# Encoder layer on one core: w_down with 20 pairs of K-tiles in seven-product form, and a tail that adds to seeded banks

## The chip, the cores and the metric

The kernel runs on one core of a Trainium2 chip, in one launch. The metric is the device time of one execution in microseconds (us). TensorE (PE) multiplies, VectorE (DVE), ScalarE (ACT) and GpSimd (POOL) work element by element, SyncE (SP) issues DMAs, and DMA queues are issued by SP, ACT and POOL. Each engine works off its own list of instructions, and semaphores hold an instruction until its inputs are there. SBUF is the memory on the chip, with 128 partitions; the matmuls write into eight PSUM banks of 128x512 numbers each; DRAM is outside.

## The reference

One encoder layer in f32 on 512 tokens of width 2048. What matters here is its last part:

```python
h = rmsnorm(x, ffn_norm_w[l])
x = x + (jax.nn.silu(h @ w_gate[l]) * (h @ w_up[l])) @ w_down[l]     # w_gate, w_up 2048x5632, w_down 5632x2048
...
return rmsnorm(x, final_norm_w)
```

Ahead of it stand w_in, windowed attention, gated linear attention and w_out. g below is silu(gate) times up, 512 tokens by 5632. Along w_down's rows (K) it has 44 K-tiles of 128, or 22 pairs of K-tiles.

## The kernel before, in words

Each f32 operand of a matmul is split into a high and a low part (`hi` is a cast on ACT, `lo` a subtraction on DVE), and each product becomes three matmuls: high by high, high by low, low by high. That is the conventional form: one K-tile, 128 tokens and 512 columns take 3 matmuls of 128x512.

The seven-product form (Winograd's variant of Strassen's scheme) multiplies blocks of 2 by 2 with seven products instead of eight. Sums and differences of blocks are made ahead on both sides, and the seven product sums (m) are combined at the end.

- **gate/up** (class `Feed`, built on `Units`): 22 pairs j, a gate unit and an up unit each, with seven steps a unit. The weights are split in steps by `lead` (L1541 sums, L1566 casts, L1572 subtractions). At the end of an up unit, `finish` multiplies gate and up (L1735 and L1742, 128x1024 on DVE) and POOL writes g of the pair to DRAM as `gd[j]` (L1744).
- **w_down, first part**: four jobs, one for each 512 columns c, on K-tiles 0 to 3 in conventional form (L348 to L350). Their results are multiplied by the norm's factor and added to the residual stream in DRAM (`xd`) by POOL DMAs.
- **w_down, seven-product part** (class `Down`): 16 pairs in four chunks, K-tiles 4 to 35. A chunk has 28 steps of 12 matmuls (L2073 to L2075): two column halves C, seven products, two duos of pairs. `make` reads g back from `gd` on SP and makes the operands T13, T24, F2 and B11 with their high and low parts (L1981 to L1997). After a product's last duo, `evac` copies its two banks to SBUF (L2118, L2120), and a POOL DMA adds them to `md` in DRAM. In the last chunk `fetch` reads `md` back, `put_back` copies it into the banks before the product starts (L2109, L2111), and the sums end in SBUF. `combine` (L2142) then makes the outputs y from the seven sums.
- **w_down, later jobs**: four jobs on K-tiles 36 to 39, conventional, on banks that `seed` has filled with y (L2159 on ACT). `residual` (L1897 on DVE) multiplies a bank by the norm's factor and adds it to x1 in SBUF.
- **tail** (`finish`, its function `run`): K-tiles 40 to 43, conventional. For each 128 tokens t and each 512 columns c there is a group of 12 matmuls (L2288 to L2290) on an empty bank, then `residual` (L1897), then `squares` (L523, ACT, with the row sum read out). After the four groups of a t, `later` makes the reciprocal root (L384 on DVE, L387 and L388 on ACT, L390 to L393 on DVE), scales (L2279) and writes out. The last group (t = 3, c = 3) goes in two halves of 256 columns (`last`, L2303 to L2322).

Nothing reorders instructions: each engine's order is the order in which the code issues them. Work slots in SBUF come from two pools, `s2` (128x512, 36 of them, tiles named a) and `s4` (128x1024, 33, named b). PSUM banks (`ps`) are given out in turn. In the trace a tile is named by the letter of its pool.

## Time and profile before

| | |
|---|---|
| median of 3 runs | 2141.14 us (2140.68 to 2141.53) |
| profiled execution, its own time | 2141.47 us |
| its span | 2139.7 us |
| gate/up to its end | 1695.7 us from the span's start |
| w_down, K-tiles 0 to 3 | 1695.7 to 1739.2 |
| w_down, seven-product part | 1739.3 to 2043.9 |
| w_down, K-tiles 36 to 39 | 2043.9 to 2088.0 |
| tail, K-tiles 40 to 43 | 2088.1 to 2131.9 |
| last output written | 2139.7 |

The stages are read off PE's timeline, by the lines of its matmuls. In the rows that follow, "L2290" is a line of the code above, "ps<-b,a" are the tiles written and read, and a row of the timeline begins with the start, counted from the span's start, and the duration. A row of the groups by line has the shapes, the count, and behind the bars the busy time in us and the mean of one in ns, then the idle time of the engine just ahead of them and what ended it.

### The profile page before, as it was taken

What the parts mean: (1) busy time and instruction counts of PE and PEld (TensorE: products, weight loads), DVE (VectorE), ACT (ScalarE), POOL (GpSimd) and SP (SyncE); (2) the same over time, 40 slices, a digit from 0 to 9 for tenths busy, and PEclk for the clock granted to TensorE, in tenths of its full rate; (3) what the DMA queues carried; (4) which work ended last, traced back from release to release, by engine and by line L of the source; (5) the groups of instructions that cost most, each with busy time, mean ns of one, the idle gap of its engine ahead of it and who ended that gap; (6) DMA issues with size and microseconds to landing.
All of it is one profiled execution on the core that took longest, in us unless ns stands there. A gap on an engine that the chain in (4) does not pass through costs nothing.

```text
span 2139.7 us, 30612 instructions
## 1 busy us (share of the span) xinstructions
PE 2128.3 (99%) x11418; PEld 1831.6 (86%) x11418; DVE 1732.0 (81%) x2361; ACT 1224.1 (57%) x2051; POOL 181.4 (8%) x294
## 2 busy tenths in 40 slices
PE   9999999999999999999999999999999999999998
PEld 7888888888888889988888888888888888888887
DVE  6688888778877568888888888888888888887885
ACT  8454445477776546455555555445555566666762
POOL 0000000122222000000000000000000010332000
PEclk9999999999999999999999999999999999999999
DMA  6644554647664233534444343344343596999572
GB/s 205 178 129 129 141 141 131 190 146 214 186 200 123 92 128 100 152 115 123 124 125 122 109 138 116 114 125 128 115 124 107 193 254 236 209 247 248 189 254 79
DMA packets 340849, 330.46 MB, mean 154 GB/s; under 512 B 15389, under 2 KB 260621, under 8 KB 340702
## 3 DMA queue, kind: packets, MB, share of 16 engines
q1 hardware_dynamic: 313598, 258.07, 39.3%
q0 software_dynamic: 26784, 69.91, 12.7%
q8 instruction: 90, 1.47, 0.3%
q10 hardware_dynamic: 320, 0.53, 0.1%
q14 instruction: 57, 0.47, 0.1%
HBM read 267.55 MB, written 60.92 MB: 154 GB/s over the span
## 4 chain that ended last, share of the span: by engine, by line
PE 95%; DMA 1%; issue 1%; ACT 1%; DVE 1%; POOL 0%; SPq 0%; DVEq 0%; POOLq 0%; ACTq 0%
PE ps L1604 35%; PE ps L1607 18%; PE ps L350 6%; PE ps L349 6%; PE ps L348 6%; PE ps L2074 5%; PE ps L2075 5%; PE ps L2073 5%; PE ps L699 1%; PE ps L2290 1%; PE ps L2289 1%; PE ps L2288 1%; PE ps L643 1%; PE ps L1702 1%; PE ps L1701 1%
## 5 line engine op out<-in xcount | busy, mean ns | idle before, releaser
L1572 DVE TENSOR_TENSOR b<-b,b 128x1024 fp32r<-128x1024 f32 x406 | 496.2, 1222 | 99.8 <-ACT b L1566 98.5
L1566 ACT CAST b<-b 128x1024 fp32r<-128x1024 f32 x406 | 421.2, 1052 | 21.1 <-DMA b<-in_w_in_dram 14.9
L1604 PE MATMUL ps<-a,b 128*128 128x512 f32 x1656 | 424.5, 392 | 0.1
L1604 PE MATMUL ps<-b,b 128*128 128x512 f32 x1592 | 421.0, 393 | 0.0
L1604 PEld LDWEIGHTS ps<-a,b 128*128 128x128 f32 x1656 | 304.4, 188 | 62.6 <-ACT ps L1638 0.3
L1604 PEld LDWEIGHTS ps<-b,b 128*128 128x128 f32 x1592 | 280.3, 189 | 42.5
L1541 DVE TENSOR_TENSOR b<-b,b 128x1024 f32<-128x1024 f32 x232 | 282.8, 1219 | 12.6 <-DMA b<-in_w_in_dram 12.5
L1607 PEld LDWEIGHTS ps<-b,b 128*128 128x128 f32 x1592 | 232.6, 190 | 23.4
L1607 PE MATMUL ps<-b,b 128*128 128x256 f32 x1592 | 242.9, 282 | 0.0
L1607 PE MATMUL ps<-a,b 128*128 128x256 f32 x1656 | 242.6, 283 | 0.0
L1607 PEld LDWEIGHTS ps<-a,b 128*128 128x128 f32 x1656 | 224.7, 191 | 8.3
L1632 ACT COPY b<-ps 128x256 f32<-128x256 f32 x126 | 46.9, 373 | 250.8 <-PE ps L1607 228.8
L2049 DVE TENSOR_TENSOR b<-b,b 128x1024 fp32r<-128x1024 f32 x112 | 136.5, 1221 | 36.0 <-ACT b L2041 36.0
L348 PE MATMUL ps<-b,b 128*128 128x512 f32 x344 | 139.1, 404 | 0.2 <-ACT b L462 0.2
L350 PE MATMUL ps<-b,b 128*128 128x512 f32 x344 | 134.6, 391 | 0.2 <-DVE b L466 0.2
L349 PE MATMUL ps<-b,b 128*128 128x512 f32 x344 | 134.4, 391 | 0.0
L2041 ACT CAST b<-b 128x1024 fp32r<-128x1024 f32 x112 | 116.6, 1052 | 25.4 <-DVE b L2029 13.1
L220 DVE TENSOR_TENSOR b<-b,b 128x512 fp32r<-128x512 f32 x120 | 79.4, 684 | 18.1 <-ACT b L239 17.9
L2073 PE MATMUL ps<-b,a 128*128 128x512 f32 x240 | 93.4, 389 | 0.0
L2074 PE MATMUL ps<-b,a 128*128 128x512 f32 x240 | 93.4, 389 | 0.0
L2075 PE MATMUL ps<-b,a 128*128 128x512 f32 x240 | 93.4, 389 | 0.0
L348 PE MATMUL ps<-a,b 128*128 128x512 f32 x216 | 86.7, 401 | 0.0
(311 smaller groups left out, 3596.4 us busy)
## 6 DMA issues: line engine op xcount, KB each, us to landing
b<-in_w_in_dram SPq DMA_DIRECT2D x94, 512.0 KB, 5.3
b<-in_w_gate_dram SPq DMA_DIRECT2D x88, 512.0 KB, 4.3
b<-in_w_up_dram SPq DMA_DIRECT2D x88, 512.0 KB, 3.8
b<-in_w_down_dram SPq DMA_DIRECT2D x88, 512.0 KB, 7.2
b<-in_w_out_dram SPq DMA_DIRECT2D x32, 512.0 KB, 4.7
md<-a POOLq DMA_DIRECT2D x56, 256.0 KB, 6.9
gd<-b POOLq DMA_DIRECT2D x22, 512.0 KB, 5.3
b<-gd SPq DMA_DIRECT2D x22, 512.0 KB, 5.1
```

Source lines behind the costliest of these rows:

```text
L348: mm(o, xh.t[:, c], wh.t[:, w], start=first and not on, stop=False, skip_group_check=on)
L349: mm(o, xh.t[:, c], wl.t[:, w], start=False, stop=False, skip_group_check=on)
L350: mm(o, xl.t[:, c], wh.t[:, w], start=False, stop=last, skip_group_check=on)
L1541: tt = lambda o, x_, y_: dve.tensor_tensor(o.t, x_.t, y_.t, op=OP.add)
L1566: act.copy(hi.t, home[key].t)
L1572: dve.tensor_tensor(lo.t, home[key].t, hi.f, op=OP.subtract)
L1604: mm(o.rearrange("p (s t) -> p s t", s=2), hi.t[:, q], self.xs[q][self.ORDER[n]], start=new and q == 0, stop=False, skip_group_check=True)
L1607: mm(o[:, 0:256], lo.t[:, q], self.xs[q][self.ORDER[n]][:, 0], start=False, stop=q == NP - 1, skip_group_check=True)
L2049: dve.tensor_tensor(lo.t, s.t, hi.f, op=OP.subtract)
L2073: mm(o, xh[:, t], wh, start=new and j == 0, stop=False, skip_group_check=True)
L2074: mm(o, xh[:, t], wl, start=False, stop=False, skip_group_check=True)
L2075: mm(o, xl[:, t], wh, start=False, stop=last and j == 1, skip_group_check=True)
```

## The change

- w_down's seven-product part takes 20 pairs in five chunks (K-tiles 0 to 39), 140 steps of 12 matmuls. The jobs on K-tiles 0 to 3 and 36 to 39 are gone. The tail keeps K-tiles 40 to 43 in conventional form.
- `prepare` makes the operands of a pair (the arithmetic of the old `make`) and writes high and low parts to DRAM, `gx[j]`, by POOL. For pairs 0 to 11 it runs in gate/up, right behind the product of gate and up, and g itself is not written; for pairs 12 to 19 `make` reads `gd` (now by POOL) and runs it in w_down. `fill` reads the operands back by POOL, kind by kind, as slots come free.
- The product sums stay in SBUF: `evac` copies the banks to `m`, and `put_back` copies `m` into the banks at the start of each product from the second chunk on. `md`, its transfers and `fetch` are gone. The order of the products within a chunk differs.
- In the tail `products` first copies y into the bank on ACT (L2232), and all matmuls add to it. The groups come in the order (t 0, 1 by c 0, 1), (t 0, 1 by c 2, 3), then t 2 and 3.
- x1 is loaded, g's last four K-tiles are split, the final norm's weights are loaded and the tail's weights are split within the last 14 steps (`ending`). The activation table of the reciprocal root is loaded between the last step and the tail.
- Gate/up holds at most 7 raw weight quads instead of 8.

```diff
+PAIRS, EARLY, FEED = 20, 12, 7
...
+        gx = dr.tile([PAIRS, P, 3584], F32, name="gx")
+        def prepare(q, f):
+            n1, f2 = f.t[:, 1], f.t[:, 0]
+            T = two(F32)
+            t13, t24 = T[0].t, T[1].t
+            tt(t13[:, a], n1[:, z], n1[:, a], op=OP.subtract)
+            tt(t13[:, z], f2[:, z], n1[:, z], op=OP.add)
+            tt(t24[:, a], f2[:, z], t13[:, a], op=OP.add)
+            tt(t24[:, z], t24[:, a], f2[:, a], op=OP.subtract)
+            yield
+            for src, col, n, done in ((f2, 512, 512, ()), (n1[:, a], 0, 256, (f,)), (t13, 1536, 512, ()),
+                                      (t24, 2560, 512, T), (None, 0, 0, ())):
...
+                        tt(lo, x_, hf, op=OP.subtract)
...
+                        pool.dma_start(out=d, in_=os_[0].flat)
...
+                    put(*os_, *gone)
...
+                    act.activation(hi, src, AF.Copy, scale=sign)
+                    yield
...
-                    pool.dma_start(out=gd[j], in_=c_.t.rearrange("p f t -> p (f t)"))
-                    put(c_)
+                    if j < EARLY:
+                        yield
+                        yield from prepare(j, c_)
+                    else:
+                        pool.dma_start(out=gd[j], in_=c_.t.rearrange("p f t -> p (f t)"))
+                        put(c_)
...
             def evac(self, ch, C, n, banks):
+                if not ch:
+                    self.m.setdefault(C, {})[n] = two(F32, 1)
+                for bank, y in zip(banks, self.m[C][n]):
...
                     put(bank)
-                    if ch == self.end:
-                        continue
-                    if ch:
-                        pool.dma_start(out=md[14 * C + 2 * n + h], in_=y.t, accum_op=OP.add)
...
-        dn = Down([[2, 4], [6, 8], [10, 12], [14, 16]])
+        dn = Down([[4 * n, 4 * n + 2] for n in range(PAIRS // 4)])
...
+            ORDER = [(t, 2 * C + c) for C in range(2) for t in range(2) for c in range(2)] + \
+                [(t, c) for t in (2, 3) for c in range(4)]
...
             def products(b, t, c, cols):
                 tok = slice(t * P, (t + 1) * P)
+                y = dn.y[c // 2][t // 2][c % 2][t % 2]
+                act.copy(b.t[:, cols], y.t[:, cols])
...
-                    mm(b.t[:, cols], xh.t[:, tok], wh.t[:, cols], start=k == 0, stop=False)
+                    mm(b.t[:, cols], xh.t[:, tok], wh.t[:, cols], start=False, stop=False, skip_group_check=True)
...
+                for t, c in ORDER:
...
+                    products(b, t, c, slice(0, 512))
+                    residual(c, t, b)
+                    squares(c, t, x1[c], ss2 if t < 3 else ss1[:, 0:4], 0 if t == 3 else 4 * t)
```

How the instructions stand now, at three places. ScalarE in the tail before, over the first two token tiles (L523 the squares of a group, L387 and L388 the reciprocal root):

```order
L523 ACTIVATE a_826_19763,small<-a_803_19356 128x512
L523 ACTIVATE a_828_19780,small<-a_807_19458 128x512
L523 ACTIVATE a_830_19797,small<-a_811_19574 128x512
L523 ACTIVATE a_832_19814,small<-a_821_19691 128x512
L387 ACTIVATE small<-small 128x1
L388 ACTIVATE small<-small 128x1
L523 ACTIVATE a_834_19847,small<-a_804_19357 128x512
L523 ACTIVATE a_836_19864,small<-a_808_19459 128x512
```

ScalarE in the tail after, from the fifth group on (L531 the squares, L2232 the copy of y into the next group's bank, L395 and L396 the reciprocal root):

```order
L531 ACTIVATE a_850_20027,small<-a_831_19689 128x512
L2232 COPY ps_746_20030<-b_1700_17172 128x512
L531 ACTIVATE a_852_20045,small<-a_833_19739 128x512
L395 ACTIVATE small<-small 128x1
L396 ACTIVATE small<-small 128x1
L2232 COPY ps_747_20064<-a_758_17071 128x512
L531 ACTIVATE a_854_20079,small<-a_832_19690 128x512
L2232 COPY ps_748_20082<-b_1700_17172 128x512
```

A copy into a bank now stands between the squares of one group and those of the next, and behind the root where there is one. TensorE at the border of two tail groups, with what it waits for, before:

```order
L2288 MATMUL ps_745_19749<-b_2017_19569,b_2022_19606 128x512
L2289 MATMUL ps_745_19749<-b_2017_19569,b_2022_19606 128x512
L2290 MATMUL ps_745_19749<-b_2017_19569,b_2022_19606 128x512
L2288 MATMUL ps_746_19766<-b_2019_19594,b_2005_19489 128x512 [waits DVE_49]
L2289 MATMUL ps_746_19766<-b_2019_19594,b_2005_19489 128x512
```

and after, at the group that the second copy above seeds:

```order
L2240 MATMUL ps_745_20006<-b_2068_19972,b_2033_19665 128x512
L2241 MATMUL ps_745_20006<-b_2068_19972,b_2033_19665 128x512 [waits DVE_49]
L2242 MATMUL ps_745_20006<-b_2068_19972,b_2033_19665 128x512
L2240 MATMUL ps_746_20030<-b_2069_19987,b_2024_19605 128x512 [waits Activation_49]
L2241 MATMUL ps_746_20030<-b_2069_19987,b_2024_19605 128x512 [waits DVE_49]
```

The first matmul of a group waited for DVE, which makes the low parts of the weights; it now waits for ACT, which makes the bank's first content. DVE in a pair of gate/up before, around the product of gate and up (L1742):

```order
L1572 TENSOR_TENSOR b_939_10556<-b_936_10532,b_938_10554 128x1024
L1742 TENSOR_TENSOR b_927_10476<-b_927_10476,b_906_10300 128x1024
L1572 TENSOR_TENSOR b_941_10581<-b_910_10325,b_940_10579 128x1024
L1541 TENSOR_TENSOR b_936_10532<-b_936_10532,b_910_10325 128x1024
L1572 TENSOR_TENSOR b_943_10605<-b_902_10272,b_942_10602 128x1024
```

and after (L1786 is the product, L1616 and L1585 the weights' split and sums, L1333 to L1346 the new work):

```order
L1786 TENSOR_TENSOR b_926_10609<-b_926_10609,b_905_10419 128x1024
L1616 TENSOR_TENSOR b_940_10713<-b_912_10480,b_939_10711 128x1024
L1333 TENSOR_TENSOR a_606_10732<-b_926_10609 128x256
L1334 TENSOR_TENSOR a_606_10732<-b_926_10609 128x256
L1335 TENSOR_TENSOR a_607_10733<-b_926_10609,a_606_10732 128x256
L1336 TENSOR_TENSOR a_607_10733<-a_607_10733,b_926_10609 128x256
L1585 TENSOR_TENSOR b_935_10665<-b_935_10665,b_912_10480 128x1024
L1616 TENSOR_TENSOR b_942_10743<-b_902_10388,b_941_10740 128x1024
L1691 TENSOR_TENSOR ps_445_10770<-a_608_10738,ps_442_10709 128x512
L1616 TENSOR_TENSOR b_946_10774<-b_935_10665,b_945_10772 128x1024
L1346 TENSOR_TENSOR a_610_10762<-b_926_10609,a_609_10761 128x512
```

The operands' sums come ahead of weight splits that stood directly behind the product, and the subtractions follow between later splits.

## The prediction

> **What bounds the kernel now.** I read the page first, for the busiest engine and the chain of waits, then the windows of 50 us for what each stage leaves free, then the timeline where the change cuts in. First the page: TensorE's (PE's) busy time, the shares of the chain, and the issue row of g's write.

> ```profile
> PE 2128.3 (99%) x11418; PEld 1831.6 (86%) x11418; DVE 1732.0 (81%) x2361; ACT 1224.1 (57%) x2051; POOL 181.4 (8%) x294
> ...
> PE 95%; DMA 1%; issue 1%; ACT 1%; DVE 1%; POOL 0%; SPq 0%; DVEq 0%; POOLq 0%; ACTq 0%
> ...
> gd<-b POOLq DMA_DIRECT2D x22, 512.0 KB, 5.3
> ```

> PE is busy 99% of the span and carries 95% of the chain. So the time is the number of matmuls times their pitch, plus the moments in which PE has nothing to start. Both are to be counted. The windows give PE, PEld, DVE, ACT and POOL busy time with instruction counts, the granted clock, the DMA share and GB/s: one stretch of gate/up, two of seven-product w_down, then the jobs on K-tiles 36 to 39 with the start of the tail, and the tail with the end.

> ```profile
> 1300.00:1350.00 50.00, 50.00 (x288) 44.04 (x287) 43.42 (x48) 24.76 (x35) 1.06 (x2) 1.00 0.37 108
> ...
> 1950.00:2000.00 50.00, 50.00 (x222) 41.39 (x222) 35.62 (x32) 34.90 (x51) 7.09 (x9) 1.00 0.97 291
> 2000.00:2050.00 50.00, 50.00 (x222) 41.41 (x221) 38.52 (x45) 39.64 (x62) 2.24 (x4) 1.00 0.60 203
> 2050.00:2100.00 50.00, 49.68 (x219) 40.79 (x218) 39.39 (x63) 24.52 (x48) 0.00 (x0) 1.00 0.45 155
> ```

> PE is full in the first three and loses 0.32 us in the fourth. DVE and ACT have room everywhere, in gate/up DVE the least: 6.6 us of 50.

> **Term 1, matmuls removed.** The pitch of a 128x512 matmul, from the timeline of PE, at the first row of the K-tile 36 to 39 jobs and 60 matmuls later:

> ```profile
> 2043.90 0.39 PE L348 MATMUL ps<-b,b 128*128 128x512 f32 x1
> ...
> 2057.50 0.39 PE L348 MATMUL ps<-b,b 128*128 128x512 f32 x1
> ```

> 13.60 us by 60 is 0.2267 us. Before, w_down's body is 192 matmuls on K-tiles 0 to 3, 112 steps of 12 and 192 on K-tiles 36 to 39: 1728. After, it is 140 steps of 12: 1680. The tail has 192 in both. 48 x 0.2267 = **10.9 us** less.

> **Term 2, a stall that goes.** The 0.32 us stand where the first later weights were split late:

> ```profile
> 2060.22 0.39 PE L348 MATMUL ps<-b,a 128*128 128x512 f32 x1
> ...
> 2060.92 0.50 PE L349 MATMUL ps<-b,a 128*128 128x512 f32 x1 [0.32 <-DVE b L220]
> ...
> 2061.26 0.40 PE L350 MATMUL ps<-b,a 128*128 128x512 f32 x1
> ```

> From start to start it is 0.70 and 0.34 instead of 2 x 0.23, so **0.6 us** goes with those jobs. The row also prices a restart: a matmul that had to wait is followed 0.34 later, 0.11 more than the pitch.

> **Term 3, operands made in gate/up.** For each of the first 12 pairs, after the product of gate and up, DVE gets four 256-wide and three 512-wide operations and one 256-wide subtraction, ACT four casts. The rows of these forms in w_down, with the price of one, and the product of gate and up in two consecutive pairs:

> ```profile
> L1996 ACT CAST a<-a 128x512 fp32r<-128x512 f32 x14 | 8.0, 621 | 0.0
> L1993 ACT ACTIVATE a<-b 128x256 fp32r<-128x256 f32 x11 | 4.6, 419 | 0.0
> ...
> L1997 DVE TENSOR_TENSOR a<-a,a 128x512 fp32r<-128x512 f32 x14 | 9.0, 686 | 4.9 <-ACT a L1996 4.9
> L1994 DVE SCALAR_TENSOR_TENSOR a<-b,a 128x256 fp32r<-128x256 f32 x11 | 4.6, 421 | 3.6 <-ACT a L1993 3.6
> ...
> 1307.34 1.22 DVE L1742 TENSOR_TENSOR b<-b,b 128x1024 f32<-128x1024 f32 x1
> ...
> 1346.45 1.22 DVE L1742 TENSOR_TENSOR b<-b,b 128x1024 f32<-128x1024 f32 x1
> ```

> That is 5 x 0.42 + 3 x 0.69 = 4.2 us of DVE and about 2.3 of ACT (three of 0.62, one of 0.42) in a pair of 39.1 us. DVE's present load there is 43.42/50 x 39.1 = 34.0; with it 38.2, still below 39.1. ACT goes from 19.4 to 21.7. The work hides, on condition that within the one unit where it falls (half a pair: 17.0 + 4.2 = 21.2 against 19.6) the split weights stay ahead; the excess of 1.6 us is less than one step's 2.8 (19.6/7), and a step's weights are split at least one step ahead. The g write on POOL (512 KB, landing in 5.3) becomes 1.75 MB in four to seven issues on the same queue, which holds nothing else there; the DMA engines move 108 GB/s there and 291 in w_down, so there is room. I take 0. If the cover goes, each of 12 pairs pays the 1.6: 0 to 19 us, nearer 0 since DVE's sum fits.

> **Term 4, the body of w_down.** Per two steps (24 matmuls, 5.44 us) ACT has two casts, two seed copies and two evacuations. Before's last chunk has this mix already:

> ```profile
> 1999.95 1.27 ACT L2120 COPY b<-ps 128x512 f32<-128x512 f32 x2 [1.23 <-PE ps L2075]
> 2001.11 1.05 ACT L2041 CAST b<-b 128x1024 fp32r<-128x1024 f32 x1
> 2002.06 1.11 ACT L2111 COPY ps<-b 128x512 f32<-128x512 f32 x2
> 2003.10 1.05 ACT L2041 CAST b<-b 128x1024 fp32r<-128x1024 f32 x1
> 2005.39 0.59 ACT L2120 COPY b<-ps 128x512 f32<-128x512 f32 x1 [1.24 <-PE ps L2075]
> ```

> It idles 1.24 of every 5.44 with PE full. In chunks 1 to 4 it now always looks so, and 8 pairs still made there add 32 casts (18 us) to some 60 pairs of steps, 0.3 each: it fits. DVE at 38.5 of 50 gains nothing on average. The 56 accumulating transfers on POOL, their fetches on SP and K-tile loads of two jobs go; POOL gets the reads of the prepared operands (36.7 MB in all), the reads of g, and the writes of pairs 12 to 19. In bytes, a chunk's weights (8.4 MB) and operands (7.3 MB) in 28 steps (76 us) are 206 GB/s, and the writes and reads of those 8 pairs bring it to some 270, about what the 1950 window moved. On POOL a write stands behind its subtraction and a fill behind the write; slots freed at issue make the next cast wait for a landing of about 5.3 us. Such waits I place at the start (the first weights and operands load together), at a few casts of chunks 0 and 1, and at the last 14 steps, where the combining of the product sums and the splitting of g's last four K-tiles nearly fill DVE. No row shows them; the nearest is the 0.6 us of term 2. Its price by two or three places is **1.5 us**; the ends are 0 and, for 8 pairs at 1.2 us each, 10.

> **Term 5, the seeds of the tail.** This decides. Before, a tail group of 12 matmuls starts on an empty bank. Now ScalarE first copies y into it. ACT works in the order given in the listing: squares of group n (L531), then the seed of group n+1 (L2232). The squares wait for DVE's residual, the residual for the end of group n, and the first matmul of n+1 for the seed. So PE stands idle from the end of one group to the seed of the next, whereas before it ran on. The same links, in before's timeline, around the end of a group:

> ```profile
> 2120.48 0.39 PE L2290 MATMUL ps<-b,b 128*128 128x512 f32 x1
> ...
> 2120.71 0.39 PE L2288 MATMUL ps<-b,b 128*128 128x512 f32 x1
> ...
> 2120.91 0.75 DVE L1897 SCALAR_TENSOR_TENSOR a<-ps,small,a 128x512 f32<-128x512 f32 x1 [1.97 <-PE ps L2290]
> ...
> 2121.69 0.63 ACT L523 ACTIVATE a<-a 128x512 f32<-128x512 f32 x1 [2.00 <-DVE a L1897]
> ...
> 2122.23 0.19 ACT L523 ACTIVATION_READ_ACCUMULATOR a<-a 128x1 f32 x1
> ...
> 2123.07 0.20 ACT L388 ACTIVATE small<-small 128x1 f32<-128x1 f32 x1
> ...
> L1632 ACT COPY b<-ps 128x256 f32<-128x256 f32 x126 | 46.9, 373 | 250.8 <-PE ps L1607 228.8
> ...
> L2111 ACT COPY ps<-b 128x512 f32<-128x512 f32 x24 | 13.3, 590 | 2.3 <-DMA b<-md 2.3
> ...
> L176 ACT ACT_TABLE_LOAD x5 | 6.4, 1283 | 1.3 <-PEq L2378 1.2
> ```

> - An ordinary change: the accumulator is read by 2122.42, the copy ends 0.59 later at 2123.01, and PE is released some 0.04 after (as DVE is after PE: 2120.87 to 2120.91), 2123.05. It would have started at 2120.71. With 0.11 for the restart, 2.45 us. There are 12 such, the last into the half group (a 256-wide copy of 0.37, 0.2 less): 29.2.
> - After the fourth group of a token tile ACT also does the two small steps of the reciprocal root (L388's end, 2123.27) ahead of the seed: 0.85 more, 3.30 x 3 = 9.9.
> - The start: last evacuation (0.6), table load 1.28, copy 0.59, with the handovers and restart 2.9.
> - Between the halves of the last group, residual and squares of half width, rows next:

> ```profile
> 2130.89 0.48 DVE L2303 SCALAR_TENSOR_TENSOR a<-ps,small,a 128x256 f32<-128x256 f32 x1
> ...
> 2131.62 0.28 PE L2290 MATMUL ps<-b,b 128*128 128x256 f32 x1
> 2131.73 0.19 ACT L2307 ACTIVATION_READ_ACCUMULATOR a<-a 128x1 f32 x1
> 2132.01 0.21 ACT L2308 ACTIVATE ss<-ss 128x5 f32<-128x5 f32 x1
> ...
> 2135.00:2136.00 1.00, 0.00 (x0) 0.00 (x0) 0.91 (x2) 0.00 (x0) 0.00 (x0) 0.71 0.61 227
> 2136.00:2137.00 1.00, 0.00 (x0) 0.00 (x0) 0.00 (x0) 0.00 (x0) 0.00 (x0) 0.50 1.02 375
> ```

> From the residual to the end of the small squares 0.35 after 2132.01 it is 1.4, plus 0.4 for the copy and 0.4 for handovers: 2.2.

> The sum is 29.2 + 9.9 + 2.9 + 2.2 = **44.2 us**. It scales with each link; with a place at 2.2 or 2.85 it is 40 or 50. Nothing behind it gives this back: the tail ends the program, and the 7.8 us of the span after PE's last matmul (2131.62 + 0.28) stay as they are.

> That ACT takes no later instruction during such a wait is seen in the squares row: 2.00 us idle, though nothing but its own input held it. [...]

> **Sum.** The profiled run took 2141.47 (span 2139.7 and 1.8 around it), 0.3 over the median of 2141.14. On the median: 2141.1 - 10.9 - 0.6 + 1.5 + 44.2 = **2175.3**.

> **The rivals.**
> - *The seeds are hidden, faster.* It needs ScalarE to run a seed before the squares ahead of it. Without term 5 but for its start it is 2134. From the sum, the change pays while the 17 places cost under 0.6 us each (10.0/17), less than the copy alone. For it: a bank is free long before. Against: the listing's order and the 2.00 us for which the squares wait. 3%; another 2% that it just balances.
> - *A cheaper break*, a residual and a seed that overlap their neighbours' ends: 1.0 to 1.8 us a place, 2147 to 2164. 4%.
> - *The body stalls too*: gate/up late by 1 us in each of 12 pairs, or operands landing late in w_down: 12 to 25 us more, 2187 to 2200. It would need one of the two stages to run late in most pairs. For it: gate/up's DVE would have 0.9 us of 39.1 left. 12%.
> - *The clock falls in the breaks.* The last two rows above show it halved about 2135.4, 3.5 us after the last matmul ended (0.71 in that window is 1.00 for 0.42 us and 0.50 after). The longest break here is 3.3. If it fell in each, a group of 2.72 us would run at half speed: 15 x 2.7 = 41 more, 2216; after the long ones only, about 8 more. 5%. [...]

> **How the numbers follow.** 74% for the forecast, 2165 to 2187 with its own bounds (terms 4 and 5). The range adds the lower part of the stalls: 2165 to 2192 leaves out 7% below and some 11% above. No change means within 0.2%, 4.3 us, about what this measurement can tell: 2%. Faster 3%, slower 95%.

> **What would show it.** In after: idle before PE's L2240 put down to ACT L2232, 40 to 50 us summed over 17 places; L2232 itself starting right behind the squares, and the squares L531 waiting for DVE L1930; the tail from first to last matmul near 85 us (43.5 of matmuls and the breaks); the stretch of w_down before it 381 us with PE full; the clock 1.00 through the tail; the first step of w_down at the same time as now. The forecast is wrong if L2232 starts before the residual of the group ahead, if PE shows gaps above 3 us in w_down, or if w_down begins over 2 us later.

## The result, and the profile after

The changed kernel takes 2226.2 us (2225.8 to 2228.1) against 2140.9 in the runs beside it: 1.040 times as long, 95% interval 1.0382 to 1.0418. The forecast was 2175.3, with 2192 as the upper end: the sign was right, the size was not, since 85 us were lost and 34 foretold.

The profiled execution has a span of 2224.5 us, 84.8 more than before. Its page, PE's busy time and the chain of waits:

```profile
PE 2155.8 (97%) x11370; PEld 1843.8 (83%) x11370; DVE 1755.1 (79%) x2381; ACT 1286.5 (58%) x2152; POOL 237.4 (11%) x442
...
PE 90%; DMA 4%; issue 3%; ACT 2%; DVE 2%; POOL 0%; DVEq 0%; ACTq 0%; POOLq 0%
```

PE now stands idle for 3% of the span, and DMA has 4% of the chain, where it had 1%. The windows of 50 us (columns as before) show where:

```profile
1700.00:1750.00 50.00, 45.61 (x195) 37.35 (x194) 38.21 (x43) 27.32 (x38) 5.42 (x10) 0.93 0.75 261
1750.00:1800.00 50.00, 44.27 (x179) 35.08 (x178) 31.07 (x34) 26.37 (x39) 15.13 (x28) 0.93 0.68 246
...
1950.00:2000.00 50.00, 44.60 (x190) 36.45 (x190) 30.89 (x28) 32.61 (x49) 4.46 (x9) 0.93 0.55 192
...
2100.00:2150.00 50.00, 33.85 (x106) 24.20 (x105) 23.73 (x41) 18.77 (x39) 0.00 (x0) 0.81 0.09 29
2150.00:2200.00 50.00, 33.73 (x94) 24.50 (x92) 14.90 (x31) 9.25 (x25) 0.00 (x0) 0.75 0.17 63
```

A full window of w_down has 222 matmuls. Three have 179 to 195, and the tail has 94 to 106. The column behind POOL's counts is the granted clock: it is below 1.00 in each of these windows, down to 0.75 in the tail. What PE waited for, in total, times and the longest:

```profile
PE ps L2240 <- ACT ps L2232: 38.1, 17, 3.0
PE ps L2087 <- DVE b L2055: 5.6, 3, 4.4
PE ps L2086 <- ACT ps L2104: 5.4, 1, 5.4
PE ps L2086 <- ACT b L2047: 4.5, 2, 3.1
PE ps L1648 <- ACT ps L1689: 2.5, 1, 2.5
PE ps L1648 <- DVE a L1698: 1.5, 1, 1.5
```

The first row is the tail's seeds (17 places, 38.1 us), the next three are w_down, the last two gate/up. With PE's first and last rows of the stages

```profile
1701.83 0.40 PE L2086 MATMUL ps<-b,a 128*128 128x512 f32 x1
...
2106.51 0.39 PE L2088 MATMUL ps<-b,b 128*128 128x512 f32 x1
...
2109.53 0.50 PE L2240 MATMUL ps<-b,b 128*128 128x512 f32 x1 [2.63 <-ACT ps L2232]
...
2215.84 0.41 PE L2242 MATMUL ps<-b,b 128*128 128x256 f32 x1
```

the account by stage is as follows (w_down's body ends one pitch behind its last start, at 2106.74).

| stage, us | before | after | difference | forecast |
|---|---|---|---|---|
| to the end of gate/up | 1695.7 | 1701.8 | +6.1 | 0 |
| w_down ahead of the tail | 392.4 | 404.9 | +12.5 (-11.5 and 24.0 of breaks) | -10.0 |
| tail, with its start | 43.8 | 109.5 | +65.7 | +44.2 |
| behind PE's last matmul | 7.8 | 8.25 | +0.4 | 0 |

### The profile page after: what moved, and what is told of

It reads as the page before. It is cut to its first block, busy times and chain, and to the rows that moved or that the text cites. A ratio compares the mean times of both kernels' runs of the same rounds, so it can differ in the third digit from the quotient of the medians.

```text
span 2224.5 us, 30882 instructions
## 1 busy us (share of the span) xinstructions
PE 2155.8 (97%) x11370; PEld 1843.8 (83%) x11370; DVE 1755.1 (79%) x2381; ACT 1286.5 (58%) x2152; POOL 237.4 (11%) x442
## 4 chain that ended last, share of the span: by engine, by line
PE 90%; DMA 4%; issue 3%; ACT 2%; DVE 2%; POOL 0%; DVEq 0%; ACTq 0%; POOLq 0%
PE ps L1648 33%; PE ps L1651 17%; PE ps L356 5%; PE ps L358 5%; PE ps L357 5%; PE ps L2087 5%; PE ps L2086 5%; PE ps L2088 5%; PE ps L2240 1%; DMA gx<-a 1%; PE ps L707 1%; PE ps L2241 1%; PE ps L2242 1%; PE ps L651 1%; PE ps L1746 1%
## 5 line engine op out<-in xcount | busy, mean ns | idle before, releaser
L1616 DVE TENSOR_TENSOR b<-b,b 128x1024 fp32r<-128x1024 f32 x406 | 495.7, 1221 | 84.5 <-ACT b L1610 82.3
L1610 ACT CAST b<-b 128x1024 fp32r<-128x1024 f32 x406 | 422.3, 1049 | 38.8 <-DMA b<-in_w_in_dram 15.1
L1648 PE MATMUL ps<-a,b 128*128 128x512 f32 x1656 | 425.5, 392 | 0.1
L1648 PE MATMUL ps<-b,b 128*128 128x512 f32 x1592 | 421.6, 393 | 4.0 <-ACT ps L1689 2.5
L1648 PEld LDWEIGHTS ps<-b,b 128*128 128x128 f32 x1592 | 280.4, 189 | 46.9 <-ACT ps L1689 2.7
L1585 DVE TENSOR_TENSOR b<-b,b 128x1024 f32<-128x1024 f32 x232 | 282.6, 1218 | 12.8 <-DMA b<-in_w_in_dram 12.8
L2055 DVE TENSOR_TENSOR b<-b,b 128x1024 fp32r<-128x1024 f32 x140 | 170.7, 1222 | 94.2 <-ACT b L2047 89.0
L2047 ACT CAST b<-b 128x1024 fp32r<-128x1024 f32 x140 | 146.1, 1048 | 32.0 <-DVE b L2035 10.9
L2086 PE MATMUL ps<-b,b 128*128 128x512 f32 x416 | 162.3, 390 | 0.0
L2087 PE MATMUL ps<-b,b 128*128 128x512 f32 x416 | 162.0, 389 | 0.0
L2088 PE MATMUL ps<-b,b 128*128 128x512 f32 x416 | 161.8, 389 | 0.0
L1354 POOL DMA_DIRECT2D gx<-a x112 | 60.6, 543 | 504.2 <-ACT a L1365 346.3
L356 PE MATMUL ps<-b,b 128*128 128x512 f32 x260 | 106.7, 410 | 0.0
L358 PE MATMUL ps<-b,b 128*128 128x512 f32 x260 | 102.1, 393 | 0.0
L357 PE MATMUL ps<-b,b 128*128 128x512 f32 x260 | 101.9, 392 | 0.0
L2116 ACT COPY a<-ps 128x512 f32<-128x512 f32 x100 | 57.8, 587 | 59.9 <-PE ps L2088 43.6
## 6 DMA issues: line engine op xcount, KB each, us to landing
b<-in_w_in_dram SPq DMA_DIRECT2D x94, 512.0 KB, 5.3
b<-in_w_gate_dram SPq DMA_DIRECT2D x88, 512.0 KB, 5.3
b<-in_w_up_dram SPq DMA_DIRECT2D x88, 512.0 KB, 4.8
b<-in_w_down_dram SPq DMA_DIRECT2D x88, 512.0 KB, 5.9
b<-gx POOLq DMA_DIRECT2D x52, 512.0 KB, 7.6
b<-in_w_out_dram SPq DMA_DIRECT2D x32, 512.0 KB, 4.6
```

The source lines that it names most:

```text
L356: mm(o, xh.t[:, c], wh.t[:, w], start=first and not on, stop=False, skip_group_check=on)
L357: mm(o, xh.t[:, c], wl.t[:, w], start=False, stop=False, skip_group_check=on)
L358: mm(o, xl.t[:, c], wh.t[:, w], start=False, stop=last, skip_group_check=on)
L1585: tt = lambda o, x_, y_: dve.tensor_tensor(o.t, x_.t, y_.t, op=OP.add)
L1610: act.copy(hi.t, home[key].t)
L1616: dve.tensor_tensor(lo.t, home[key].t, hi.f, op=OP.subtract)
```

## The experiments

The theories: **A**, the tail's breaks are the waits for the seeds, and the breaks bring the clock down; **E**, in w_down ACT waits for slots whose write to `gx` has not landed; **H**, w_down's start lacks DMA bandwidth; its rival there, the loads lack slots. The runs of the kernel before beside these kernels had medians of 2141.2 to 2141.4.

### The seeds one group ahead

```diff
 for g, (t, c) in enumerate(ORDER):
+    seed(g)
+    seed(g + 1)          # act.copy of y into the next group's bank
     products(...)        # no copy in it
     residual(c, t, b)
     squares(c, t, ...)
```

> The changed kernel with one edit: y is copied into the bank of group n+1 before the matmuls of group n are issued, so on ScalarE the seed stands ahead of group n's squares. Theory A (the wait for the seed makes the breaks, and the breaks make the clock fall): both go, the tail shrinks from 109.5 us to about 48 (43.6 of matmuls, 2.6 of start, one slow clock window at the start at most), the clock is 1.00 from then on, and the time falls by about 61 us to 2165. Rival B (the seeded banks or the late weight splits slow the tail in themselves): PE still waits between groups, for DVE's split weights, and the time stays above 2190. Rival C (the clock falls for its own reason in the tail): breaks gone, clock still halved in many windows, about 2188.

2174.4 us (2171.8 to 2174.9), 51.8 less than the changed kernel. Its clock is 1.00 in the tail but for one stretch of 3.4 us behind the start (0.97 on the mean from 2106.9 to 2165 us, against 0.75 over the changed kernel's tail). So theory A holds in kind: the seeds made the breaks, and the clock came back with them; rival C falls. But 61 were expected, and a part of rival B is true. PE's wait in the tail, and a group border:

```profile
PE ps L2251 <- ACT ps L2240: 10.1, 9, 2.6
```

and its timeline:

```profile
2118.21 0.63 ACT L531 ACTIVATE a<-a 128x512 f32<-128x512 f32 x1 [1.50 <-DVE a L1930]
...
2118.84 0.58 ACT L2240 COPY ps<-a 128x512 f32<-128x512 f32 x1
2119.36 1.13 ACT L247 CAST b<-b 128x512 fp32r<-128x512 f32 x2
2119.47 0.50 PE L2251 MATMUL ps<-b,b 128*128 128x512 f32 x1 [0.38 <-ACT ps L2240]
2120.00 1.29 DVE L228 TENSOR_TENSOR b<-b,b 128x512 fp32r<-128x512 f32 x2 [1.82 <-ACT b L247]
...
2121.21 0.74 DVE L1930 SCALAR_TENSOR_TENSOR a<-ps,small,a 128x512 f32<-128x512 f32 x1
```

A second loop stands behind the first: squares, seed, the casts of two weight splits, their subtractions on DVE, and only then the next residual, which the next squares wait for. It takes 3.8 us a group (2117.43 to 2121.21 from residual to residual), longer than 12 matmuls (2.72).

### The breaks filled with matmuls that nobody reads

```diff
     mm(b.t[:, cols], xl.t[:, tok], wh.t[:, cols], start=False, stop=k == per - 1, ...)
+if cols.start == 0:
+    spare = ps.get()
+    for _ in range(8):
+        mm(spare.t, xh.t[:, tok], wh.t, start=True, stop=True)
+    put(spare)
```

> The changed kernel, seeds as they are, but behind each group of the tail PE runs 8 matmuls of 128x512 into a spare bank that nobody reads (added work, 1.8 us of each break of 2.1). The waits for the seeds stay. Theory A (a window of 3.4 us with too little matmul work halves the next one): the clock stays 1.00 through the tail, a group and its break take 5.07 us instead of 6.6, the tail is about 83 us instead of 109.5 and the time falls by some 26 us to 2200, although 128 matmuls were added. Rival D (the lost time beyond the idle is the restart of a waiting PE, not the clock): no gain, 2226 or somewhat more.

2205.1 us (2201.9 to 2207.0): 21.1 less, with 128 matmuls more. Here is the tail's middle, 80 us of it:

```profile
2110.00:2190.00 80.00, 73.41 (x311) 55.99 (x310) 31.05 (x59) 24.01 (x61) 0.00 (x0) 1.00 0.11 40
```

and the wait for the seeds that is left:

```profile
PE ps L2240 <- ACT ps L2232: 9.2, 15, 2.6
```

The clock is 1.00. The seeds come no sooner: 9.2 us of idle and 16 fillings of 1.81 make 38.2, as before. So of the tail's 65.7 some 21 us were the clock and 38 the idle time at the seeds; the 6 or 7 left, restarts behind 17 breaks among them, were not taken apart. Rival D falls. A row of windows, cut along the clock's own steps, shows in the changed kernel how the clock went; the first number behind the length is PE's busy time:

```profile
2113.79:2117.20 3.41, 1.33 (x6) 0.85 (x5) 1.21 (x2) 2.24 (x5) 0.00 (x0) 1.00 0.00 0
2117.20:2120.61 3.41, 3.41 (x9) 2.35 (x8) 0.84 (x2) 0.03 (x1) 0.00 (x0) 0.50 0.00 0
2120.61:2124.03 3.42, 1.34 (x6) 0.93 (x6) 1.35 (x2) 2.28 (x5) 0.00 (x0) 1.00 0.00 0
```

Here every second window is at half clock (16 of the tail's 32): in one at full clock PE works 1.3 us and waits 2.1; the next runs at half clock, with the matmuls 0.43 us apart instead of 0.23, and PE is busy in more of it (here all of it, elsewhere in the tail 2.2 to 3.4 us); then the clock comes back, behind 14 of the 16.

### Two filling matmuls instead of eight

> As fill8 with 2 added matmuls per break instead of 8 (0.45 us of each 2.1). It asks where the clock's threshold lies: in the changed kernel windows of 3.41 us in which PE worked 0.39 or less were followed by half clock, those with 0.50 or more were not; with 2 added matmuls the emptiest windows have about 0.45. If the gate goes by the share of work in a window with a threshold between 0.39 and 0.45, the clock stays 1.00 and the time is that of fill8, 2203 to 2206. If it lies between 0.45 and 0.50, about half of the windows still fall, 2212 to 2218. If it needs PE busy all the time, 2226.

2206.9 us (2206.7 to 2207.1), 1.8 above the kernel with eight: 0.9 above the first branch of the expectation and well below the second. PE still waits 30.8 us for the seeds in 17 places, 2.6 at the longest, and yet the clock stays: only two windows of the tail fell, one at the start (the table load) and one that holds nearly all of a wait of 2.5 us behind a root (ended at 2153.97). Two more waits of 2.5 us, ended at 2142.91 and 2176.77, lay across the border of two windows, and neither window fell. The view of this kernel:

```profile
2151.72:2155.13 3.41, 1.16 (x5) 0.98 (x6) 1.94 (x9) 1.61 (x5) 0.00 (x0) 1.00 0.00 0
2155.13:2158.54 3.41, 3.41 (x10) 2.63 (x9) 1.85 (x3) 0.00 (x0) 0.00 (x0) 0.50 0.60 220
2168.78:2172.20 3.42, 1.79 (x8) 1.18 (x7) 0.73 (x1) 1.21 (x3) 0.00 (x0) 1.00 0.00 0
```

From 1699 us to the end of the tail, in the changed kernel and this one, 268 such windows began at full clock. In 22 PE was busy 1.54 us or less: each was followed by half clock. In 246 it was busy 1.72 or more: none was. So in these two traces the windows part by PE's busy time, between 0.45 and 0.50 of 3.41 us as this view counts, and none of the 22 was without work: the emptiest had 0.40 us. (The expectation counts from start to start of the matmuls. So counted, the fullest of the 22 and the emptiest of the 246 have about 0.40 and 0.42, since the view's durations are longer than the pitch, 0.39 against 0.23.)

### All operands made in gate/up

```diff
-PAIRS, EARLY, FEED = 20, 12, 7
+PAIRS, EARLY, FEED = 20, 20, 7
```

> The changed kernel with EARLY = 20: the operands of all 20 pairs are made in gate/up, none in w_down. Theory E (in w_down ACT waits for slots whose last use is a write to gx that has not landed): the breaks at 1759 to 1764, 1780 to 1784 and 1958 to 1963 us go, 11.1 us of idle and two stretches of 6.8 us at half clock, together 17 to 18 us; the break at the start of w_down (4.4 idle) and those in the first units of gate/up stay, and the 8 further pairs hide in gate/up: about 2208. Rival F (the reads of the prepared operands are what is late): the breaks stay where they are, 2222 to 2230. Rival G (gate/up's DVE cannot hide 8 more pairs): gate/up ends 5 us or more later.

2209.0 us (2207.9 to 2210.4), 17.2 less: theory E, and gate/up hides 8 more pairs (w_down begins 0.9 us earlier, if anything). PE's waits from 1690 us on are two rows, the tail's seeds and the start of w_down:

```profile
PE ps L2240 <- ACT ps L2232: 38.2, 17, 3.0
PE ps L2087 <- DVE b L2055: 4.3, 1, 4.3
```

In the changed kernel the three places that have gone looked like this on ACT and DVE:

```profile
1760.78 0.42 ACT L1365 ACTIVATE a<-b 128x256 fp32r<-128x256 f32 x1 [7.55 <-DMA gx<-a]
...
1781.38 0.59 ACT L2116 COPY a<-ps 128x512 f32<-128x512 f32 x1 [9.72 <-DMA gx<-a]
...
1961.95 1.04 ACT L2047 CAST b<-b 128x1024 fp32r<-128x1024 f32 x1 [8.39 <-DMA gx<-b]
...
1963.55 0.79 PE L2086 MATMUL ps<-b,a 128*128 128x512 f32 x1 [5.40 <-ACT ps L2104]
```

A cast or an evacuation into a slot that a write to `gx` still reads waited 7.6 to 9.7 us here, and the weights' casts stand behind it on ACT or are that cast. The chain of waits has the write as one piece, from issue to landing, here at the second and the third place:

```profile
1768.64 12.64 DMA gx<-a
...
1950.85 11.02 DMA gx<-b
```

12.6 us for a write of 256 KB and 11.0 for one of 512 KB, while the page has a median of 3.8 for the writes of 256 KB,

```profile
gx<-a POOLq DMA_DIRECT2D x132, 256.0 KB, 3.8
```

and around the third place POOL alone issued eight reads of operands from 1948.5 to 1954.6, beside four loads of weights by SP up to 1958.

### The start of w_down and pair 0 as well

```diff
 if u == len(self.units) - 1:
     ...
-    self.fill((6, 6, 6, 4, 4, 6, 4)[n], 2)
+    self.fill((6, 6, 6, 4, 4, 6, 4)[n], 2, ("T24", "F2"))   # these two kinds not yet
...
-yield from prepare(j, c_)
+for _ in prepare(j, c_):
+    yield
+    if j == 0:
+        yield
```

> As early20, and two edits more at other places: in the last unit of gate/up only the operands B11 and T13 of the first chunk are read, T24 and F2 not before w_down runs; and the operand work of pair 0 is spread over twice as many steps. Theory H (w_down's start is short of DMA bandwidth: 10.3 MB asked in 25 us) expects the break of 4.4 us with the half clock behind it at 1705 to 1714 us to shrink from 7.8 us to under 2; the spreading takes the two breaks of 4.0 us and the slow window out of gate/up's first units, some 5.5. Together about 2196. Rival: the weights are late because their SBUF slots come free late, not for bandwidth; then the start stays at 7 to 8 us lost, and the time is about 2202.

2199.7 us (2199.5 to 2199.9), 9.3 less than with EARLY alone. The first window of its w_down:

```profile
1700.00:1750.00 50.00, 50.00 (x223) 41.40 (x222) 37.30 (x34) 28.78 (x38) 5.78 (x11) 1.00 0.55 194
```

and PE's only wait between 860 and 1690 us:

```profile
PE ps L1648 <- ACT b L1610: 1.4, 1, 1.4
```

From its first to its last matmul w_down is 380.8 us, 1680 pitches without a break. What the first sums of weights waited for in the changed kernel is the first row here; the other two are from gate/up's first units:

```profile
1706.94 1.23 DVE L2032 TENSOR_TENSOR b<-b,b 128x1024 f32<-128x1024 f32 x1 [6.88 <-DMA b<-in_w_down_dram]
...
886.95 0.63 ACT L1365 ACTIVATE a<-a 128x512 fp32r<-128x512 f32 x1 [3.07 <-DVE a L1344]
...
893.01 0.69 DVE L1346 TENSOR_TENSOR a<-a,a 128x512 fp32r<-128x512 f32 x1 [2.73 <-DMA gx<-a]
```

The second row stands ahead of gate/up's first break, which PE ends at 888.11: a cast of pair 0 waits for DVE's L1344, a subtraction of the same pair that comes behind sums and splits of weights on DVE, and the ACT operation that PE needs (L1689) stands behind that cast on ACT. The third stands ahead of the second break (897.05): a subtraction of pair 0 into a slot that its own earlier write still held, with the weights' sums behind it. Pair 0 took two steps of this work per step of PE, the later pairs one; spread out, the 4.0 us of waits (3.5 with EARLY alone) become 1.4. The two profiled executions differ by 9.8 us: w_down, with the break at its start, accounts for 6.0 (386.8 to 380.8 us) and gate/up for 4.0. But the 4 MB that are asked for later would also have taken eight slots of SBUF, so this run does not tell bandwidth from slots. The next one was meant to.

### The slots taken, the reads issued later

```diff
 def fill(self, least4, least2=1, kinds=()):
+    while self.waiting and not kinds:
+        o_, i_ = self.waiting.popleft()
+        pool.dma_start(out=o_, in_=i_)
     ...
+    if kind in kinds:                   # T24 and F2, in gate/up's last unit
+        self.waiting.extend(dmas)       # the slots are taken, the reads wait for w_down
```

> As body, but in the last unit of gate/up the operands T24 and F2 of the first chunk take their SBUF slots as in the changed kernel; only their reads are issued later, in w_down's first step. It separates the two readings of body at the start of w_down. If the break of 4.4 us there came from DMA bandwidth (the 4 MB asked for ahead of the weights), it stays away: 2199 to 2201, as body. If it came from the weights' loads waiting for slots that the operands had taken, the loads are late again and the break is back with its half clock: about 2206.

2206.3 us (2205.5 to 2206.6), 6.6 more than `body`: the break is back. PE's wait at the start of w_down:

```profile
PE ps L2098 <- DVE b L2066: 4.7, 1, 4.7
```

But the run does not separate the two readings, because the edit moved the reads in the code and hardly in time. POOL, which issues them, had no reason to wait for w_down and ran ahead of PE. It issued the 11 reads of the waiting list (L1976) from 1682.2 to 1694.8 us; these are the first and the last of them:

```profile
1682.18 2.17 POOL L1976 DMA_DIRECT2D b<-gx  x4
...
1694.80 0.55 POOL L1976 DMA_DIRECT2D a<-gx  x1 [1.74 <-PE ps L1651]
```

That is 15.0 to 2.3 us ahead of w_down's first matmul; with EARLY alone the same reads went out 15.0 to 2.2 us ahead of it. So both the slots and the bytes were as there, and the break had to come back by either reading. What there is on the question is in the traces. First the first issue of w_down's weights on SP, in `held` and then in `body`:

```profile
1680.58 30.77 SPq L1970 DMA_DIRECT2D b<-in_w_down_dram  x12
```

```profile
1673.81 35.15 SPq L1969 DMA_DIRECT2D b<-in_w_down_dram  x16
```

The first load goes out 6.8 us later, since the next free slots are those that gate/up's own weight splits still read: SP waits 22.4 us there for DVE's L1616 (16.1 in `body`). The load that the break waits for goes out when another such split ends, in `held`'s chain of waits:

```profile
1690.46 1.24 DVE b L1616
...
1691.72 10.77 DMA b<-in_w_down_dram
```

It is the fifth, and it lands at 1702.5; the fifth of `body` goes out at 1685.0 and lands 8.1 us later, at 1693.1. Of these 9.4 us, 6.7 are the late issue, that is slots, and 2.7 the longer way behind the reads, that is bytes. The DMA engines were busy for 90% or more of each 0.8 us from 1688 to 1700 us in both, at 399 and 387 GB/s. An estimate from these numbers: since PE waited 4.7, the load had to land by 1697.8. Issued as in `body`, with 10.8 us on the way, it would have landed in time, at 1695.8; issued late, with 8.1 on the way, it would have been 2.0 late. So the slots look like the larger part of the break and the bytes of theory H like the smaller; no run shows either alone.

### Everything together

```diff
 if l == 11:
+    tables(EXP_LN)                      # within w_down's last steps
 if l == 13:
+    for n in range(3):
+        seed_tail(n)
...
 for g, (t, c) in enumerate(ORDER):
+    for n in (g, g + 1):
+        issue(n)                        # seeds of n to n + 2, then products(n) with its weight splits
     residual(c, t, seeded[g][0])
     squares(c, t, ...)
```

> All repairs together: the edits of body; the activation table is loaded and the first three banks are seeded within w_down's last steps; in the tail, banks are seeded three groups ahead, and the matmuls and weight splits of group n+1 are issued before the residual and the squares of group n. If the breaks and the clock are all that the change lost (theories A, E and H), PE runs from the first matmul of w_down to the last of the tail without a break: 1696.9 + 1680 x 0.2267 + 43.6 = 2121.3 on the span's clock, the end 8.3 later, 1.7 around it: 2131.3, 0.995 of the kernel before (the 10.9 us of term 1 less the 1 us that gate/up still gives away). If the tail has a second limit of its own (DVE's residuals and splits, 8 banks), it is above 2136.

> As best4, but with the order of the tail as in seed_ahead, seeds three groups ahead instead of one: the residual of a group still comes behind the subtractions of its weight splits on DVE, whose casts stand behind the previous group's squares on ACT. If this loop (0.75 + 0.8 + 0.6 + 1.1 + 0.7 and handovers, 3.8 us a group measured in seed_ahead against 2.7 of matmuls) only delays residuals, seeds three ahead cover it in the five groups that split weights: within 1 us of best4. If PE also waits for the weights that the loop delays, it is 3 to 6 us slower than best4.

With the products of a group issued ahead of the previous residual it takes 2134.7 us (2134.3 to 2135.3), 0.997 of the kernel before (0.9958 to 0.9980), 6.5 us faster. With the order of the first experiment and seeds three ahead (`best3`) it takes 2137.8 (2137.5 to 2139.9), 0.9985 (0.9976 to 0.9994): the loop of splits costs 3.1. The waits that PE keeps from 1690 us on in the faster one:

```profile
PE ps L2261 <- ACT b L247: 0.8, 1, 0.8
PE ps L2262 <- DVE b L228: 0.5, 2, 0.2
```

Of the forecast 2131.3 the tail misses 2.5 (1.3 of waits for split weights and their restarts: its matmuls run from 2077.3 to 2123.4), and the end behind PE, 9.1 us, another 0.8.

## Why the prediction was wrong, step by step

- **Terms 1 and 2** were right. In the kernel `body` 1680 matmuls take 380.8 us without a break, 10.9 less than 1728, and the stall at 2060 is gone with its jobs.
- **Term 5** was right in place, mechanism and size. The idle time was 38.1 us in 17 places. The links at an ordinary border, in the timeline of after:

```profile
2120.86 0.75 DVE L1930 SCALAR_TENSOR_TENSOR a<-ps,small,a 128x512 f32<-128x512 f32 x1 [2.83 <-PE ps L2242]
...
2121.65 0.63 ACT L531 ACTIVATE a<-a 128x512 f32<-128x512 f32 x1 [4.42 <-DVE a L1930]
...
2122.28 0.58 ACT L2232 COPY ps<-a 128x512 f32<-128x512 f32 x1
...
2122.91 0.50 PE L2240 MATMUL ps<-b,b 128*128 128x512 f32 x1 [2.08 <-ACT ps L2232]
```

  2.08 of idle where the working had 2.18 ahead of the restart, 2.9 to 3.0 behind a root, 2.6 at the start, 1.8 between the halves. The tail's 65.7 less the clock's 21 is 44.6, where the term had 44.2.
- **The rival of the clock** is the first step that failed. It got 5%, with 3.3 us as the longest break against the 3.5 after which the clock was seen halved behind the last matmul. That figure came from one event, where PE was wholly idle, so it tells nothing of a window that is half empty. In the changed kernel's tail the windows of 3.41 us that half clock followed had PE busy for 0.85 to 1.54 us. The clock cost some 21 us; the price given for it, 41, assumed half speed in every group, while 16 of the tail's 32 windows were at half clock, and 14 of those were followed by full clock.
- **Term 4** is the second, sized at 1.5 with 0 to 10 as its ends, and 24.0 in fact. It named the start and the casts of chunk 0, where three of the four breaks came, and the waits for slots; the fourth came in chunk 3, and none in the last 14 steps, which it also named. What failed is the price: it took a landing at 5.3, the median of a write of g with little beside it. The writes that ACT waited for behind reads took 12.6 and 11.0 at two of the places, the breaks were 2.2 to 5.4 us of idle, not 1.2, and three of the four brought the clock down for 6.8 us each. The first break, at the start, was of another kind: with the reads of T24 and F2 left for w_down it is gone. The weights' loads went out late for want of slots, which the term did not count, and were long on the way behind the operands' bytes, which it named; how much each did stays open.
- **Term 3**, sized at 0, was 6.1. DVE's load did fit, with 20 pairs too. What failed is the step that counted work and no waits: pair 0's casts and subtractions wait for each other and for slots whose writes are under way, and the weights' splits stand behind them. Spread over twice the steps, most of it went.

The clock alone (21 us) or term 4 alone (22.5 more than its 1.5) would have carried the time past the 2192 of the range. Two of the signs that the prediction named for being wrong came true: gaps above 3 us in w_down, and w_down 6.1 us later. Two small slips in it change nothing: its chances below the range add up to 9% (3, 2 and 4), not 7, and the read-out of the small squares ends 0.30 behind 2132.01, not 0.35.

## What to carry to other kernels

When an engine gets a new task that TensorE waits for, look at what stands ahead of it in its list: here a copy of 0.6 us cost 2.1, since it stood behind squares that waited for the matmuls themselves; issued three groups ahead, with the matmuls ahead of the residual, it cost no wait. Count breaks twice, once as idle time and once as clock: here half clock followed the windows of 3.41 us with 1.54 us of work or less and none with 1.72 or more. Matmuls that nobody reads, placed in the breaks, made this kernel 21 us faster and serve as the test. A slot that a DMA or a split still reads is not free (ACT waited 7.6 to 9.7 us for three of them): count slots at each border of stages, and price a landing beside the transfers that will be issued around it (12.6 us here, where the median was 3.8). An issue that stands later in the code need not go out later (11 reads meant for w_down's first step went out 15.0 to 2.3 us ahead of it): read the start times before you take an edit for what it was meant to do.
